# Gate projections in another order, and q's low part written straight into two lasting buffers

## The chip, the cores and the metric

The kernel runs on one core of one Trainium2 chip. The metric is the device time of one execution in microseconds (us); the median of several executions is compared. A profile of one execution shows what each engine did: PE is TensorE (matmuls), PEld its weight loads, DVE VectorE, ACT ScalarE, POOL GpSimd, SP SyncE, which here only issues DMAs.

## What is computed

The block takes x of shape (1, 1024, 1024), with sequence length S = 1024 and width D = 1024:

```python
h = _rmsnorm(x, norm_g)
u = h @ w_in                       # RWKV columns, attention columns, 2048 gate columns
y = wkv7_scan(r, decay, k, v, -kk, kk * a)      # 8 heads of 64, a recurrence over 1024 steps
a_out = (groupnorm(y) + bonus) * silu(gate_a)
q, k = _rmsnorm(q), _rmsnorm(k)                 # 8 heads of 64
logits = q @ k.T * scale + cum[q] - cum[k]      # cum: running sum of log_sigmoid(f)
b_out = softmax(causal(logits)) @ v * silu(gate_b)
m = sigmoid(gate_1) * (a_out @ w_out_a) + sigmoid(gate_2) * (b_out @ w_out_b)
out = _rmsnorm(x + m @ w_out, final_norm_g)
```

Everything is fp32. The matmuls take each operand as a high and a low part (names with H and L): high times high, high times low and low times high, three matmuls for one product.

## The kernel before

**Bulk work.** `project` multiplies one 128-column block of weights with the transposed, normed input `hTH`/`hTL` for one half n of the sequence: 24 matmuls of 512 columns into one PSUM tile. `mix` uses it for RWKV columns (with the token shift), `gate_tile(j)` for the gates: j = 16 to 19 are RWKV's gates and go through `mix`, j = 20 to 23 are attention's gates, j = 0 to 15 the 16 sigmoid gates of the final merge. What must read the PSUM tile before it is free differs. For 0 to 15 it is ACT alone (L413). For 20 to 23 it is ACT and then DVE (L417). For 16 to 19 it is ACT and then DVE (L375 and, for the first half, L381, `last_gg`), with the silu's product (L402) also on DVE. The bulk tiles rotate through three PSUM buffers, so that a tile's first matmul waits for the readers of the tile three before it. Results go to DRAM (`gab`) and come back when they are used. The weights of each block come by DMA (L225, L873, L941) into one raw buffer, are cast by ACT (L210) and their low parts made by POOL (L213).

**RWKV.** Four units (p, n), called 0_0, 0_1, 1_0 and 1_1, run in sequence. `prep` of a unit forms products `psc` (PE, L604), masks them on DVE into QL and Q (L610), scales them on POOL, sends them through DRAM into the layout `lt` (DMAs L639 and L643), inverts a triangular matrix by elimination in some sixty small steps on DVE (L680, L684, with the scratch tile `etmp`), goes through DRAM again, transposes on DVE into `TW` (L696), and multiplies on PE (`pw` L704, `pz` L717). `chain` then runs 8 steps that depend on each other (px, xw, pu, SV, po, state). `norm_out` closes the unit (the gate `yg` is loaded, POOL multiplies, L828). Bulk work lies between these pieces on PE.

**Attention.** Four pairs of heads p. `norm_qk` makes the high parts QA and KA by ACT and the low parts by DVE; QA's second copy is made by DMA (L1010, L1011). q's low part goes from DVE (`ql`, L1004) to DRAM (`qlo`, L1008); `attend` zeroes half of a tile QZ on POOL (L1030) for each of its four blocks of 256 queries and loads the other half from `qlo` (L1031). The scores `sc` are a matmul with QA (L1053), one with QZ (L1056) and a mask (L1060). The probabilities are transposed (pt), split (PHL, L1084 to 1093) and multiplied with V (po, L1099). Beside this PE runs the projections of the next pair (`pf`) and gate tiles.

**Merge.** `ring` tiles bring gates, attention results and weights; `pma` and `pmb` are bulk tiles of the output projections, freed by DVE (L1155, L1158).

**What sets the order.** A scheduler lays every engine's order in advance; each engine then runs its list in that order, and an instruction that waits holds all behind it. `PLACE` pins the first matmuls of a group behind a given count of bulk pieces ("pw1_0": 404 means not before piece 404), `SCAT` does so for the first scores of a pair, `PTAT` for the last unit's transposes. `RFILL` and `FPRE` say how many gate tiles are taken from the list `gates` beside each unit and each attention pair. Tags name memory: tiles of one tag share a buffer, and the later waits for the last reader of the earlier.

Of the kernel before, what the change touches and what calls it, by code (L numbers as in the profile page):

```python
# [9 lines left out]
F32 = mybir.dt.float32  # L10
# [8 lines left out]
P = 128  # L19
# [32 lines left out]
QKFIRST = True  # L52
LATER = 1000000
PLACE = {
    "pw0_0": 179, "pz0_0": 183, "pw0_1": 296, "pz0_1": 301, "sc1_0": 352, "pw1_0": 404, "pz1_0": 409,
    "sc1_1": 457, "pw1_1": 525, "pz1_1": 535,
}
PACE = 0.3
PHPOOL = True
# [38 lines left out]
def kernel(  # L98
# [318 lines left out]
                nc.vector.scalar_tensor_tensor(t, t, 1.0, ps, op0=ALU.add, op1=ALU.mult)  # L417
            store(n, t)

    gates = list(range(16, 24)) + list(range(16))  # L420

    def fill(n, off=LATER):
        with order(off):
# [92 lines left out]
    def prep(pp_, n):  # L516
# [43 lines left out]
        nc.vector.reciprocal(s2c, s2)  # L560

        bo = ep.tile([P, UC, 2, C], F32, tag="prod", name=f"bo{u}")
        late_sc = []
        for e in range(2):
            p, w = 2 * pp_ + e, f"{u}_{e}"
            own, other = (slice(0, C), slice(C, P))[:: 1 - 2 * e]
            ta, th = ew(f"ta{w}"), ew(f"th{w}")
            nc.sync.dma_start(flat(th), lod[0, p, :, HS[n]])
            nc.sync.dma_start(flat(ta), lod[1, p, :, HS[n]])
            sg = ew(f"sg{w}")  # L570
            nc.vector.memset(pad(sg)[:, :, 0:1], 0.0)
            nc.vector.tensor_scalar(pad(sg)[:, :, 1:], ch(th), 0.5, 0.5, op0=ALU.mult, op1=ALU.add)
            cum = ew(f"cum{w}")
            nc.vector.tensor_tensor_scan(
                cum, d0.rearrange("p c t -> p (c t)"), sg, 0.0, op0=ALU.mult, op1=ALU.add
            )
            E = ew(f"E{w}")
            nc.scalar.activation(E, cum, AF.Exp, scale=-KAPPA)
            Ei = ew(f"Ei{w}")
            nc.scalar.activation(ch(Ei), pad(cum)[:, :, 1:], AF.Exp, scale=KAPPA)  # L580
            nc.vector.tensor_copy(WC[:, e], pad(E)[:, :, C])

            BK = ep.tile([P, UC, P], F32, tag="lt", name=f"BK{w}")
# [12 lines left out]
            nc.vector.scalar_tensor_tensor(bo[:, :, e], ch(ta), cs("rk", p), ch(rx[e]), op0=ALU.mult, op1=ALU.mult)


            for h, q in ((0, A), (1, B)):
                for g in range(2):  # L600
                    psc = ps_misc(f"psc{w}_{g}_{h}")
                    for j in range(4):
                        c = 4 * g + j
                        ins = nc.tensor.matmul(  # L604
                            psc[:, j * P : (j + 1) * P], BK[q, c, :], AR[q, e, c, :], start=True, stop=True
                        )
                        if e:
                            late_sc.append(ins.ins)
                    for cols, m, dst in ((own, 0, QL), (other, C, Q)):
                        nc.vector.tensor_mul(  # L610
                            dst[:, e, h, 4 * g : 4 * g + 4, :],
                            psc.rearrange("p (c t) -> p c t", t=P)[:, :, cols],
                            mask[:, m : m + C].unsqueeze(1).broadcast_to([P, 4, C]),
                        )
            for g in range(2):
                pb = ps_misc(f"pb{w}_{g}")
                for j in range(4):
                    nc.tensor.transpose(pb[:, j * P : (j + 1) * P], BK[:, 4 * g + j, :], ident)
                nc.scalar.copy(BKt[:, e, 4 * g : 4 * g + 4].rearrange("p c i -> p (c i)"), pb)
# [52 lines left out]
                        )  # L672
            nc.scalar.copy(AK[:, 4 * g : 4 * g + 4].rearrange("p c i -> p (c i)"), pk)

        etmp = rp.tile([4 * NG, 2, 256], F32, tag="etmp", name=f"etmp{u}")
        nc.vector.memset(lt[:, 0 : HB * HB : HB + 1], 1.0)
        for s in range(1, HB - 1):
            m = HB - 1 - s
# [8 lines left out]
        for e, _, *qs in half:  # L687
            for i, q in enumerate(qs):
                for h in range(2):
                    nc.sync.dma_start(  # L690
                        Tg[q, h, :, q], td[e, i, UC * h : UC * h + UC].transpose([1, 0, 2])
                    )
        TW = rp.tile([P, HALF], F32, tag="TW", name=f"TW{u}").rearrange("p (g t) -> p g t", t=HB)
        for e, _, q1, q2 in half:
            for h in range(2):
                nc.vector.transpose(TW[q1, UC * h : UC * h + UC, :], Tg[q1, h, :, q1])  # L696
# [23 lines left out]
                    )  # L720
        for e, _, q1, q2 in half:
            nc.scalar.copy(Tg[q1, :, :, q2], pz[q1, :].rearrange("p (h c t) -> p h c t", h=2, t=HB))
        return dict(pz=pzs, AR=AR, Q=Q, BKt=BKt, SV=SV, AK=AK, WC=WC, bV=bV, s2c=s2c, lnw=lnw, pw=mms, sc=late_sc, pt=[])

    states = [rp.tile([P, 2, 2, C], F32, tag=f"state{j}", name=f"state{j}") for j in range(2)]
    for t in states:
# [2 lines left out]
    def chain(pp_, n, d):  # L729
# [1 line left out]
        u = f"{pp_}_{n}"  # L731
        pairs = ((0, A, B), (1, B, A))
        yv = rp.tile([P, UC, 2, C], F32, tag="yw", name=f"yv{u}", bufs=YWB)
        xw = rp.tile([P, 4, P], F32, tag="xw", name=f"xw{u}")
        for c in range(UC):
            gc = UC * n + c
            st_c, st_n = states[gc % 2], states[1 - gc % 2]
# [58 lines left out]
    def norm_out(pp_, n, d, yv):  # L796
# [26 lines left out]
                )  # L823
        for e in range(2):
            p = 2 * pp_ + e
            yg = rp.tile([P, HALF], F32, tag="yg", name=f"yg{u}_{e}")
            nc.sync.dma_start(yg, gab[16 + p, :, HS[n]])
            nc.gpsimd.tensor_mul(yo[:, e], yo[:, e], yg)  # L828
            nc.sync.dma_start(yab[p, :, HS[n]], yo[:, e])
# [146 lines left out]
    def norm_qk(p, xn, rr):  # L976
# [2 lines left out]

        KA = (rp if p % 2 else qp).tile([P, 2, S], F32R, tag=("Q", "AR")[p % 2], name=f"KA{p}")  # L980
        QA = rp.tile([P, 2, S], F32R, tag=("QL", "BKt")[p % 2], name=f"QA{p}")
        qlo = dp.tile([P, S], F32, tag="qlo", name=f"qlo{p}", bufs=2)

        def half(n, places):
            xg = xn[n].rearrange("p b (g i) -> p (b g) i", i=HD)
            (nc.gpsimd if n in NORMPOOL else nc.vector).tensor_mul(xg, xg, rr[n].unsqueeze(2).broadcast_to([P, 16, HD]))
            for c, key in ((1, "k"), (0, "q")):
# [7 lines left out]
                hi = KA if key == "k" else QA  # L995
                for h, q, qo in halves:
                    nc.scalar.activation(hi[q, h, HS[n]], pq[q], AF.Copy, scale=1.0 if key == "k" else gqk[q])
                if key == "q":
                    ql = rp.tile([P, HALF], F32R, tag=("TW", "etmp")[n], name=f"ql{p}_{n}")
                for h, q, qo in halves:  # L1000
                    if key == "k":
                        nc.vector.tensor_sub(KA[qo, h, HS[n]], pq[q], hi[q, h, HS[n]])  # L1002
                    else:
                        nc.vector.scalar_tensor_tensor(  # L1004
                            ql[q], pq[q], gqk[q], hi[q, h, HS[n]], op0=ALU.mult, op1=ALU.subtract
                        )
                if key == "q":
                    nc.sync.dma_start(qlo[:, HS[n]], ql.bitcast(F32))  # L1008
            QAf = QA.bitcast(F32)[:, :, HS[n]]
            nc.sync.dma_start(QAf[B, 0], QAf[A, 0])  # L1010
            nc.sync.dma_start(QAf[A, 1], QAf[B, 1])  # L1011

        return KA, QA, qlo, half

    sc_tags = SCTAGS

    blocks = [[] for _ in range(4)]

    def attend(p, KA, QA, qlo):
        cb = [rp.tile([P, S], F32, tag=("AK", "bV")[h], name=f"cb{p}_{h}") for h in range(2)]  # L1020
        for h in range(2):
            src = cumd[8 * (2 * p + h) : 8 * (2 * p + h) + 8].rearrange("(o b) t -> o (b t)", o=1)
            nc.sync.dma_start(cb[h], src.broadcast_to([P, S]))
        for i in range(4):
            nb = 2 * i + 2

            QZ = rp.tile([P, 2, QB], F32R, tag=("yg", "xw")[i % 2], name=f"QZ{p}_{i}")
            QZf = QZ.bitcast(F32)
            for h, q, qo in ((0, A, B), (1, B, A)):
                nc.gpsimd.memset(QZf[qo, h, :], 0.0)  # L1030
                nc.sync.dma_start(QZf[q, h, :], qlo[q, i * QB : (i + 1) * QB])  # L1031
            yo = rp.tile([P, QB], F32, tag="state0", name=f"yo{p}_{i}")
            yg = rp.tile([P, QB], F32, tag="state1", name=f"yg{p}_{i}")
            nc.sync.dma_start(yg, gab[20 + p, :, i * QB : (i + 1) * QB])
            for h, q in ((0, A), (1, B)):
# [3 lines left out]
                for e in range(2):  # L1039
# [6 lines left out]
                    for g in range(ng):  # L1046
# [7 lines left out]
                        if e == 0 and g == 0:  # L1054
                            blocks[p].append(qk.ins)
                        nc.tensor.matmul(  # L1056
                            sc[:, :mw], QZ[:, h, e * P : (e + 1) * P], KA[:, h, ms], start=False, stop=not end
                        )
                        if end:
                            nc.tensor.matmul(sc[:, gw - P : gw], identb, cmask, start=False, stop=True)  # L1060
# [69 lines left out]
    def merge():  # L1130
# [9 lines left out]
        with tc.tile_pool(name="yp", bufs=1, side="right", reuse_waits="tile") as yp:  # L1140
# [46 lines left out]
    for i, (p, n) in enumerate(units):  # L1187
# [3 lines left out]
        with bulky():  # L1191
# [3 lines left out]
            fill(RFILL[i], 0)  # L1195
            if i + 1 == len(units):
                project_v(0)
                forget()
                xr = project_qk(0)
        not_before(d["pw"], f"pw{p}_{n}")  # L1200
        not_before(d["pz"], f"pz{p}_{n}")
        not_before(d["sc"], f"sc{p}_{n}")
        if i:
            not_before(before["pt"], "pt%d_%d" % units[i - 1])
# [9 lines left out]

    def next_qk(p, xr, between=lambda: None):

        KA, QA, qlo, half = norm_qk(p, *xr)
        starts.append(len(laid_) - 1)
        half(0, QKAT[0])
        between()  # L1220
        with order(LATER) if p == 0 else nullcontext():
            gate_tile(gates.pop(0))
        half(1, QKAT[1])
        return KA, QA, qlo

    def last_norm():
        with order(-LATER):
# [15 lines left out]
    for p in range(4):  # L1243
        end = starts[p + 1] if p < 3 else len(laid_) - 1
        room = sum(cols_[starts[p] + 1 : end + 1]) - SCAT * HALF
        for k, first in enumerate(blocks[p]):
            i, h = divmod(k, 2)
            if k == 0 or SPREAD:
                pins.append(([first], starts[p], int(SCAT * HALF + SPREAD * room * (i + h) * (i + 1) / 20)))
    bulk_tags[:] = TTAGS  # L1250
    tc.cur_priority += LATER
    place_all()
    mH, mL, wos = merge()
# [65 lines left out]
```

## Time and profile before

| | |
|---|---|
| median of 3 runs | 1120.16 us (1118.36 to 1122.01) |
| the profiled execution | 1110.45 us |
| its span in the profile | 1108.4 us |
| mean granted clock of TensorE | 0.981 of full speed |
| busy: PE, DVE, ACT, POOL | 1044.7, 703.9, 460.1, 320.9 us |

The span is what the profile covers; the 2 us beside it lie before and after. The profiled execution was 9.7 us shorter than the median of the timed runs.

### The profile page before, as it was taken

How to read it: one execution, taken by the hardware profiler on the slowest of the kernel's cores; microseconds unless marked ns; L12 is line 12 of the kernel's file. 1: busy time of each engine (PE TensorE's matmuls, PEld its weight loads, DVE VectorE, ACT ScalarE, POOL GpSimd, SP SyncE). 2: the span in 40 equal slices, each digit the busy share in tenths (PEclk: the TensorE clock that was granted, in tenths of full speed). 3: DMA queues.
4: the chain of work that ended last, by engine and by line, in shares of the span. 5: the costliest groups of instructions: out<-in, count | busy, mean ns of one | idle time of the engine just before them, and what ended most of it. 6: DMA issues, size and time to landing. Idle time of an engine off the chain costs nothing. (4 is left out here: it accounts for less than half of the span.)

```text
span 1108.4 us, 18398 instructions
## 1 busy us (share of the span) xinstructions
PE 1044.7 (94%) x6591; PEld 866.8 (78%) x6591; DVE 703.9 (64%) x1855; ACT 460.1 (42%) x969; POOL 320.9 (29%) x467
## 2 busy tenths in 40 slices
PE   4989999998999998999989899899999899999996
PEld 3867788776778776778979788787899687887885
DVE  7414775699737873597466595785764685475145
ACT  6545323533243323423353564665453563233122
POOL 4531522234222531143120422323222322335300
PEclk9999999999999899999979899999999999999999
DMA  6266434224522343223211512313232416645133
GB/s 218 56 185 219 133 96 124 62 74 121 146 89 60 114 126 113 59 56 107 71 39 51 153 51 76 106 48 97 63 109 58 130 51 205 192 141 190 51 102 123
DMA packets 126685, 118.21 MB, mean 107 GB/s; under 512 B 33490, under 2 KB 91971, under 8 KB 126595
## 3 DMA queue, kind: packets, MB, share of 16 engines
q1 hardware_dynamic: 114304, 94.99, 29.6%
q10 hardware_dynamic: 11714, 21.52, 5.2%
q8 instruction: 52, 0.85, 0.3%
q0 software_dynamic: 576, 0.54, 0.2%
q14 instruction: 39, 0.31, 0.1%
HBM read 79.23 MB, written 35.68 MB: 104 GB/s over the span
## 5 line engine op out<-in xcount | busy, mean ns | idle before, releaser
L348 PE MATMUL ps_gg<-hTH,wH_gg 128*128 128x512 f32 x384 | 159.3, 415 | 7.0 <-DVE last_gg L381 4.4
L350 PE MATMUL ps_gg<-hTH,wL_gg 128*128 128x512 f32 x384 | 156.6, 408 | 0.0
L349 PE MATMUL ps_gg<-hTL,wH_gg 128*128 128x512 f32 x384 | 156.1, 406 | 0.0
L213 POOL TENSOR_TENSOR wL_gg<-w_gg,wH_gg 128x256 fp32r<-128x256 f32 x96 | 75.3, 815 | 191.6 <-ACT wH_gg L210 146.0
L348 PEld LDWEIGHTS ps_gg<-hTH,wH_gg 128*128 128x128 f32 x384 | 73.4, 191 | 24.1 <-issue 5.4
L350 PEld LDWEIGHTS ps_gg<-hTH,wL_gg 128*128 128x128 f32 x384 | 73.3, 191 | 14.9
L349 PEld LDWEIGHTS ps_gg<-hTL,wH_gg 128*128 128x128 f32 x384 | 73.4, 191 | 14.0
L959 PE MATMUL pf<-wqkH,hTH 128*128 128x256 f32 x256 | 74.7, 292 | 0.2 <-DVE KA L1002 0.2
L960 PE MATMUL pf<-wqkL,hTH 128*128 128x256 f32 x256 | 74.6, 291 | 0.0
L961 PE MATMUL pf<-wqkH,hTL 128*128 128x256 f32 x256 | 74.4, 291 | 0.0
L758 ACT ACTIVATE xw<-state,WC 64x64 f32<-64x64 f32 x112 | 38.9, 348 | 44.0 <-DVE state L778 34.7
L1066 ACT ACTIVATE pr<-pr,mm 128x128 f32<-128x128 f32 (+3 forms) x64 | 50.0, 782 | 17.2 <-DVE mm L1062 16.4
L680 DVE TENSOR_TENSOR etmp<-lt 64x30 f32<-64x30 f32 (+14 forms) x120 | 47.8, 398 | 10.7 <-issue 7.1
L1062 DVE CUSTOM_DVE_ANT_0 pr<-sc,cb 128x128 f32<-128x128 f32 (+3 forms) x64 | 34.0, 534 | 30.8 <-PE sc L1060 24.1
L413 ACT ACTIVATE gt<-ps_gg 128x512 f32<-128x512 f32 x40 | 23.9, 599 | 70.8 <-PE ps_gg L350 63.5
L1273 PE MATMUL pz<-wo,mH 128*128 128x512 f32 (+1 forms) x136 | 51.9, 382 | 0.9 <-POOL wo L1128 0.9
L1274 PE MATMUL pz<-wo,mL 128*128 128x512 f32 (+1 forms) x136 | 52.3, 385 | 0.0
L1272 PE MATMUL pz<-wo,mH 128*128 128x512 f32 (+1 forms) x136 | 51.7, 380 | 0.0
L684 DVE TENSOR_TENSOR lt<-lt,etmp 64x30 f32<-64x30 f32 (+14 forms) x120 | 48.3, 402 | 3.6
L959 PEld LDWEIGHTS pf<-wqkH,hTH 128*128 128x128 f32 x256 | 49.7, 194 | 0.6 <-DVE KA L1002 0.4
L1099 PE MATMUL po<-PHL,V 128*128 128x256 f32 x160 | 46.8, 307 | 2.9 <-ACT PHL L1084 2.7
L960 PEld LDWEIGHTS pf<-wqkL,hTH 128*128 128x128 f32 x256 | 49.4, 193 | 0.0
(332 smaller groups left out, 2826.9 us busy)
## 6 DMA issues: line engine op xcount, KB each, us to landing
w_gg<-in_w_in_dram SPq DMA_DIRECT2D x24, 512.0 KB, 3.8
gab<-gt ACTq DMA_DIRECT2D x48, 256.0 KB, 2.3
ring<-gab SPq DMA_DIRECT2D x32, 256.0 KB, 3.2
xt<-in_x_dram SPq DMA_DIRECT2D x8, 512.0 KB, 5.8
wqk<-in_w_in_dram SPq DMA_DIRECT2D x16, 256.0 KB, 3.1
cb<-cumd SPq DMA_DIRECT2D x8, 512.0 KB, 4.1
ring<-yab SPq DMA_DIRECT2D x16, 256.0 KB, 3.5
ring<-in_w_out_dram SPq DMA_DIRECT2D x16, 256.0 KB, 2.8
```

The costliest lines, as they stand in the source:

```text
L213: nc.gpsimd.tensor_sub(wL[:, k], w[:, k], wH[:, k])
L348: nc.tensor.matmul(ps, wH[:, k, :], rH[:, k, ts_], start=(k == 0), stop=False)
L349: nc.tensor.matmul(ps, wH[:, k, :], rL[:, k, ts_], start=False, stop=False)
L350: laid(nc.tensor.matmul(ps, wL[:, k, :], rH[:, k, ts_], start=False, stop=(k == nk - 1)))
L684: nc.vector.tensor_add(lt3[:, :s, s + 1 :], lt3[:, :s, s + 1 :], tm)
L959: nc.tensor.matmul(ps, hTH[:, k, bs], wH[:, kk, :], start=(k == 0), stop=False)
L960: nc.tensor.matmul(ps, hTH[:, k, bs], wL[:, kk, :], start=False, stop=False)
L961: laid(nc.tensor.matmul(ps, hTL[:, k, bs], wH[:, kk, :], start=False, stop=(k == KD - 1)), QB)
L1066: nc.scalar.activation(pr[:, :w], pr[:, :w], AF.Exp, bias=last, scale=-1.0, accum_out=mm[:, 2:3])
L1272: nc.tensor.matmul(ps, mH[:, k, bs], oH[:, k, c], start=(k == 0), stop=False)
L1273: nc.tensor.matmul(ps, mH[:, k, bs], oL[:, k, c], start=False, stop=False)
L1274: nc.tensor.matmul(ps, mL[:, k, bs], oH[:, k, c], start=False, stop=(k == KD - 1))
```

## The change

The list of gates gets another order, and one gate tile is taken between v's projection and those of q and k for the last unit. Pins and counts change with it. `etmp` and `TW` become one tile (`inv`), `xw` and `yg` another (`xy`). DVE writes q's low part straight into two tiles `QZ` that take over these tags once; their other rows are zeroed once, for pair 0. The DRAM tensor `qlo`, its 8 stores, 32 loads and 32 zeroings are gone. The tag list `TTAGS` (8 PSUM buffers for bulk tiles) is set after the `pma` tiles, no longer before them; until then `FTAGS` (3 buffers) holds.

```diff
-    "pw0_0": 179, "pz0_0": 183, "pw0_1": 296, "pz0_1": 301, "sc1_0": 352, "pw1_0": 404, "pz1_0": 409,
-    "sc1_1": 457, "pw1_1": 525, "pz1_1": 535,
+    "se0_0": 113, "pw0_0": 179, "pz0_0": 183, "pw0_1": 296, "pz0_1": 301, "sc1_0": 356, "pw1_0": 408, "pz1_0": 413,
+    "sc1_1": 461, "pw1_1": 540, "pz1_1": 548,
...
-PTAT = 6
-SCAT = 16
+PTAT = 5
+SCAT = 14
...
-RFILL = [5, 5, 4, 4]
-FPRE = [0, 0, 0, 2]
+RFILL = [5, 5, 4, 3]
+FPRE = [0, 0, 1, 1]
...
-    gates = list(range(16, 24)) + list(range(16))
+    gates = [16, 17, 0, 1, 2, 3, 18, 19, 4, 5, 6, 7, 20, 21, 22, 23] + list(range(8, 16))
...
-        etmp = rp.tile([4 * NG, 2, 256], F32, tag="etmp", name=f"etmp{u}")
+        inv = rp.tile([P, 2, HALF], F32, tag="inv", name=f"inv{u}")
+        etmp = inv[: 4 * NG, 0].rearrange("p (a b) -> p a b", a=2)
...
-        qlo = dp.tile([P, S], F32, tag="qlo", name=f"qlo{p}", bufs=2)
...
-                if key == "q":
-                    ql = rp.tile([P, HALF], F32R, tag=("TW", "etmp")[n], name=f"ql{p}_{n}")
+                if p == 0 and key == "q":
+                    QZ.append(rp.tile([P, 2, HALF], F32R, tag=("inv", "xy")[n], name=f"QZ{n}"))
+                    for h, q, qo in halves:
+                        nc.gpsimd.memset(QZ[n].bitcast(F32)[qo, h, :], 0.0)
...
-                            ql[q], pq[q], gqk[q], hi[q, h, HS[n]], op0=ALU.mult, op1=ALU.subtract
+                            QZ[n][q, h, :], pq[q], gqk[q], hi[q, h, HS[n]], op0=ALU.mult, op1=ALU.subtract
...
-                if key == "q":
-                    nc.sync.dma_start(qlo[:, HS[n]], ql.bitcast(F32))
...
-            QZ = rp.tile([P, 2, QB], F32R, tag=("yg", "xw")[i % 2], name=f"QZ{p}_{i}")
-            QZf = QZ.bitcast(F32)
-            for h, q, qo in ((0, A, B), (1, B, A)):
-                nc.gpsimd.memset(QZf[qo, h, :], 0.0)
-                nc.sync.dma_start(QZf[q, h, :], qlo[q, i * QB : (i + 1) * QB])
+            QZi = QZ[i // 2][:, :, (i % 2) * QB : (i % 2 + 1) * QB]
...
+            bulk_tags[:] = TTAGS
             for c in range(KD):
                 side(w_out_b, yb, 4, "b", c, then_b)
...
                 project_v(0)
+                gate_tile(gates.pop(0))
                 forget()
                 xr = project_qk(0)
...
-    bulk_tags[:] = TTAGS
     tc.cur_priority += LATER
     place_all()
```

The laid order on DVE during the elimination of unit 0_1, before the change; `ps_gg_1978` is the first half of gate 18:

```order
L680 TENSOR_TENSOR etmp_1_2706<-lt_1_2634 64x220
L684 TENSOR_TENSOR lt_1_2634<-lt_1_2634,etmp_1_2706 64x20x11
L375 SCALAR_TENSOR_TENSOR gt_0_2005<-ps_gg_1978,col,t_gg_2003 128x511
L680 TENSOR_TENSOR etmp_1_2706<-lt_1_2634 64x210
L378 SCALAR_TENSOR_TENSOR gt_0_2005<-zcol,col,t_gg_2003 128x1
L684 TENSOR_TENSOR lt_1_2634<-lt_1_2634,etmp_1_2706 64x21x10
L381 COPY last_gg_2008<-ps_gg_1978 128x1
L680 TENSOR_TENSOR etmp_1_2706<-lt_1_2634 64x198
L402 SCALAR_TENSOR_TENSOR gt_0_2005<-gth_0_2010,gt_0_2005 128x512
L684 TENSOR_TENSOR lt_1_2634<-lt_1_2634,etmp_1_2706 64x22x9
```

The same steps of the elimination after the change, where the gate in that place is gate 0:

```order
L680 TENSOR_TENSOR inv_1_2673<-lt_1_2601 64x220
L684 TENSOR_TENSOR lt_1_2601<-lt_1_2601,inv_1_2673 64x20x11
L680 TENSOR_TENSOR inv_1_2673<-lt_1_2601 64x210
L684 TENSOR_TENSOR lt_1_2601<-lt_1_2601,inv_1_2673 64x21x10
L680 TENSOR_TENSOR inv_1_2673<-lt_1_2601 64x198
L684 TENSOR_TENSOR lt_1_2601<-lt_1_2601,inv_1_2673 64x22x9
L680 TENSOR_TENSOR inv_1_2673<-lt_1_2601 64x184
L684 TENSOR_TENSOR lt_1_2601<-lt_1_2601,inv_1_2673 64x23x8
```

The five DVE instructions of a `mix` gate between the steps have left this stretch; gates 18 and 19 now come four gates later, after 0 to 3.

PE where the chain of unit 1_1 runs and the first `pf` of q and k comes, before the change:

```order
L746 MATMUL px_1_4_5706<-state_432,AR_1_4373 128x128 x2
L761 MATMUL pu_1_4_5717<-xw_1_5595,Tb 128x64 x2
L771 MATMUL po_1_4_5722<-SV_1_4377,BKt_1_4376 128x128 x2
L746 MATMUL px_1_5_5729<-state_433,AR_1_4373 128x128 x2
L918 MATMUL pcs<-lf,tri 128x64
L919 MATMUL pcs<-lf,tri 128x64
L761 MATMUL pu_1_5_5740<-xw_1_5595,Tb 128x64 x2
L771 MATMUL po_1_5_5745<-SV_1_4377,BKt_1_4376 128x128 x2
L746 MATMUL px_1_6_5752<-state_432,AR_1_4373 128x128 x2
L761 MATMUL pu_1_6_5763<-xw_1_5595,Tb 128x64 x2
L959 MATMUL pf_0_1_5365<-wqkH_0_5314,hTH 128x256
```

And after it; `ps_gg_1_5248` is the second half of the gate tile that now stands between v and q and k:

```order
L348 MATMUL ps_gg_1_5248<-hTH,wH_gg_5211 128x512
L349 MATMUL ps_gg_1_5248<-hTL,wH_gg_5211 128x512
L350 MATMUL ps_gg_1_5248<-hTH,wL_gg_5212 128x512
L772 MATMUL po_1_2_5648<-SV_1_4364,BKt_1_4363 128x128 x2
L919 MATMUL pcs<-lf,tri 128x64
L920 MATMUL pcs<-lf,tri 128x64
L747 MATMUL px_1_3_5655<-state_433,AR_1_4360 128x128 x2
L762 MATMUL pu_1_3_5666<-xy_1_5585,Tb 128x64 x2
L772 MATMUL po_1_3_5671<-SV_1_4364,BKt_1_4363 128x128 x2
L788 MATMUL py_1_3_5678<-SV_1_4364,Q_1_4361 64x64 x16
L747 MATMUL px_1_4_5696<-state_432,AR_1_4360 128x128 x2
L762 MATMUL pu_1_4_5707<-xy_1_5585,Tb 128x64 x2
```

What has no bulk between it, before, are the chain's pieces from po_1_3 to pu_1_6 (po_1_3 and py_1_3 stand just ahead of these rows), and after the change those from po_1_2 to pu_1_4.

SP before the scores of pair 3, before the change (`w_gg` is a gate's weights, `w_oa` those of merge):

```order
L1010 DMA QA_8833<-QA_8833 64x512
L1011 DMA QA_8833<-QA_8833 64x512
L225 DMA w_gg_9529<-in_w_in_dram 128x8x128
L1008 DMA qlo_8834<-ql_0_8852 128x512
L1031 DMA QZ_0_8950<-qlo_8834 64x256 x2
L1031 DMA QZ_1_9034<-qlo_8834 64x256 x2
```

And after it:

```order
L225 DMA w_gg_8841<-in_w_in_dram 128x8x128
L225 DMA w_gg_9423<-in_w_in_dram 128x8x128
L1011 DMA QA_8817<-QA_8817 64x512
L1012 DMA QA_8817<-QA_8817 64x512
L234 DMA w_oa_9528<-in_w_out_a_dram 128x4x256
```

The store of `qlo` and the loads of QZ are gone from the queue, and so is the load of a gate's weights in front of them; merge's weights follow QA's copies directly.

## Rows read from the trace of the kernel before

**Rows 1.** The page, part 1: busy time, share of the span and instructions of each engine.

```profile
PE 1044.7 (94%) x6591; PEld 866.8 (78%) x6591; DVE 703.9 (64%) x1855; ACT 460.1 (42%) x969; POOL 320.9 (29%) x467
```

**Rows 2.** The waits of PE: total us, times, longest; after the arrow what ended them.

```profile
PE sc L1056 <- DMA QZ<-qlo: 10.9, 5, 3.2
...
PE ps_gg L348 <- DVE last_gg L381: 4.4, 2, 3.0
...
PE psc L604 <- DVE Q L610: 3.0, 2, 2.0
PE pw L704 <- DVE TW L696: 2.8, 2, 1.5
PE po L1099 <- ACT PHL L1084: 2.7, 2, 2.1
PE ps_gg L348 <- DVE gt L375: 1.6, 2, 1.2
...
PE ps_gg L348 <- DVE gt L417: 0.9, 1, 0.9
```

**Rows 3.** Windows of DVE: us and length, DVE busy (x instructions), PEclk, DMA share, GB/s.

```profile
240.00:270.00 30.00, 28.94 (x70) 0.97 0.37 96
...
313.00:350.00 37.00, 21.32 (x66) 1.00 0.28 87
...
350.00:370.00 20.00, 19.81 (x38) 1.00 0.33 97
```

**Rows 4.** Windows of PE: us and length, PE busy (x instructions), PEclk, DMA share, GB/s.

```profile
370.00:380.00 10.00, 8.00 (x47) 0.87 0.46 151
380.00:390.00 10.00, 9.71 (x78) 0.79 0.33 68
563.00:568.60 5.60, 4.12 (x50) 1.00 0.02 4
568.60:582.20 13.60, 10.72 (x44) 0.50 0.31 80
620.00:630.00 10.00, 6.82 (x32) 0.66 0.44 134
860.00:870.00 10.00, 7.37 (x51) 1.00 0.38 120
```

**Rows 5.** Timeline of PE where prep's matmuls stand: start, us, line, tile [idle before].

```profile
376.15 1.01 PE L604 MATMUL psc<-AR,BK 64*128 64x128 f32 x7 [2.00 <-DVE Q L610]
...
426.87 0.69 PE L704 MATMUL pw<-TW,Tb 32*32 32x32 f32 x32 [1.28 <-DVE TW L696]
...
541.55 1.13 PE L704 MATMUL pw<-TW,Tb 32*32 32x32 f32 x59
```

**Rows 6.** Timeline of SP, 387 to 388 us: when each DMA is issued.

```profile
387.38 0.38 SPq L524 DMA_DIRECT2D vx<-xd  x1
387.93 0.47 SPq L643 DMA_DIRECT2D lt<-ld  x1
```

**Rows 7.** Timeline of SP before the scores of pair 3.

```profile
855.66 0.39 SPq L225 DMA_DIRECT2D w_gg<-in_w_in_dram  x1
...
861.01 2.40 SPq L1031 DMA_DIRECT2D QZ<-qlo  x4
```

**Rows 8.** Timeline of PE at the first scores of pair 3.

```profile
860.40 0.28 PE L1053 MATMUL sc<-KA,QA 128*128 128x256 f32 x1
863.31 0.40 PE L1056 MATMUL sc<-KA,QZ 128*128 128x256 f32 x1 [2.63 <-DMA QZ<-qlo]
```

**Rows 9.** Timeline of DVE in merge: the additions L1155 that free the PSUM of pma.

```profile
947.63 1.28 DVE L1155 SCALAR_TENSOR_TENSOR m<-ring,pma 128x512 f32<-128x512 f32 x2
...
953.26 1.28 DVE L1155 SCALAR_TENSOR_TENSOR m<-ring,pma 128x512 f32<-128x512 f32 x2
...
961.40 0.69 DVE L1155 SCALAR_TENSOR_TENSOR m<-ring,pma 128x512 f32<-128x512 f32 x1 [2.11 <-PE pma L350]
964.20 0.69 DVE L1155 SCALAR_TENSOR_TENSOR m<-ring,pma 128x512 f32<-128x512 f32 x1 [2.11 <-PE pma L350]
```

More of the change, by code (lines that the diff above doesn't have):

```diff
@@ L562, in prep @@
         bo = ep.tile([P, UC, 2, C], F32, tag="prod", name=f"bo{u}")
-        late_sc = []
+        first_sc, late_sc = [], []
         for e in range(2):
@@ L606, in prep @@
                         )
-                        if e:
-                            late_sc.append(ins.ins)
+                        (late_sc if e else first_sc).append(ins.ins)
                     for cols, m, dst in ((own, 0, QL), (other, C, Q)):
@@ L692, in prep @@
                     )
-        TW = rp.tile([P, HALF], F32, tag="TW", name=f"TW{u}").rearrange("p (g t) -> p g t", t=HB)
+        TW = inv[:, 1].rearrange("p (g t) -> p g t", t=HB)
         for e, _, q1, q2 in half:
@@ L722, in prep @@
             nc.scalar.copy(Tg[q1, :, :, q2], pz[q1, :].rearrange("p (h c t) -> p h c t", h=2, t=HB))
-        return dict(pz=pzs, AR=AR, Q=Q, BKt=BKt, SV=SV, AK=AK, WC=WC, bV=bV, s2c=s2c, lnw=lnw, pw=mms, sc=late_sc, pt=[])
+        return dict(pz=pzs, AR=AR, Q=Q, BKt=BKt, SV=SV, AK=AK, WC=WC, bV=bV, s2c=s2c, lnw=lnw, pw=mms, se=first_sc, sc=late_sc, pt=[])
     states = [rp.tile([P, 2, 2, C], F32, tag=f"state{j}", name=f"state{j}") for j in range(2)]
@@ L733, in chain @@
         yv = rp.tile([P, UC, 2, C], F32, tag="yw", name=f"yv{u}", bufs=YWB)
-        xw = rp.tile([P, 4, P], F32, tag="xw", name=f"xw{u}")
+        d["xy"] = rp.tile([P, 2, HALF], F32, tag="xy", name=f"xy{u}")
+        xw = d["xy"][:, 0].rearrange("p (a b) -> p a b", a=4)
         for c in range(UC):
@@ L825, in norm_out @@
             p = 2 * pp_ + e
-            yg = rp.tile([P, HALF], F32, tag="yg", name=f"yg{u}_{e}")
+            yg = d["xy"][:, 1]
             nc.sync.dma_start(yg, gab[16 + p, :, HS[n]])
@@ L1011, in half, with attend @@
             nc.sync.dma_start(QAf[A, 1], QAf[B, 1])
-        return KA, QA, qlo, half
+        return KA, QA, half
     sc_tags = SCTAGS
+    QZ = []
     blocks = [[] for _ in range(4)]
-    def attend(p, KA, QA, qlo):
+    def attend(p, KA, QA):
         cb = [rp.tile([P, S], F32, tag=("AK", "bV")[h], name=f"cb{p}_{h}") for h in range(2)]
@@ L1056, in attend @@
                         nc.tensor.matmul(
-                            sc[:, :mw], QZ[:, h, e * P : (e + 1) * P], KA[:, h, ms], start=False, stop=not end
+                            sc[:, :mw], QZi[:, h, e * P : (e + 1) * P], KA[:, h, ms], start=False, stop=not end
                         )
@@ L1201 @@
         not_before(d["pz"], f"pz{p}_{n}")
+        not_before(d["se"], f"se{p}_{n}")
         not_before(d["sc"], f"sc{p}_{n}")
@@ L1215, in next_qk @@
     def next_qk(p, xr, between=lambda: None):
-        KA, QA, qlo, half = norm_qk(p, *xr)
+        KA, QA, half = norm_qk(p, *xr)
         starts.append(len(laid_) - 1)
@@ L1223, in next_qk @@
         half(1, QKAT[1])
-        return KA, QA, qlo
+        return KA, QA
     def last_norm():
```

## The prediction

> **What bounds the kernel now.** I read the page first. PE is busy for 1044.7 of 1108.4 us [rows 1]; no other engine is near that. So time can only be won where PE stands still or runs slowly, and PE's bulk work, which the change does not touch in amount, lies in a fixed order. The list of PE's waits comes next. Its largest entry is the scores' second matmul, waiting for a DMA: 10.9 us in five places, 3.2 us the longest. Then come the gates' PSUM tiles, whose readers on DVE are late (4.4, 1.6 and 0.9 us), `psc` behind DVE's Q (3.0), `pw` behind TW (2.8) and `po` behind PHL (2.7) [rows 2]. The windows of PE then show what a stop costs beside its own length. The granted clock was 0.87 and 0.79 between 370 and 390 us, 0.50 from 568.6 to 582.2, and 0.66 from 620 to 630 us, but 1.00 from 860 to 870 us, although PE was busy for only 7.37 of those 10 us [rows 4]. Last I looked at what is late behind each wait: DVE is busy for 28.94 of the 30 us from 240 to 270 and for 19.81 of the 20 from 350 to 370, but only for 21.32 of the 37 us from 313 to 350 [rows 3].
>
> **The change part by part.** All terms are in us of the profiled execution; plus is time won.
>
> *Gates 0 to 3 ahead of 18 and 19.* The bulk that lies beside unit 0_1's elimination is freed by ACT alone, where before DVE had to find room for five instructions of each half gate among the elimination's steps. The first wait of 3.0 us belongs to gate 17, which stays; the waits for gates 18 and 20 go: 4.4 − 3.0 = 1.4 for `last_gg`, 1.2 for L375, 0.9 for L417 [rows 2]. That is 3.5. Gates 18 and 19 themselves now lie where DVE has 16 us of 37 free [rows 3]. Upper bound 3.9 (all of L375's 1.6), lower bound 2, if one wait like the 1.4 comes back there. I take **+3.5**.
>
> *Unit 1_0.* Its pins move by 4 pieces, and the last gate of the moved pair puts some of its DVE work into the stretch that is already full [rows 3]. PE comes to `psc` later against its bulk, so the 2.00 us there [rows 5] shrink, and with them the slow clock behind it: 10 × 0.13 + 10 × 0.21 = 3.4 us between 370 and 390 [rows 4]. But `pw`, which waited 1.28 us at its last piece [rows 5] and 2.8 in all with the one before [rows 2], is set by a serial path: Q, POOL, a DMA, the elimination, a DMA, TW. PE that is faster in between only waits there longer. The path shortens only where PE itself is in it: `lt`'s load stands on SP behind a load of `vx` at 387.38 that follows a product of PE [rows 6], and that product comes earlier by what the slow clock took. So between 0 and 3.4; I take **+2**.
>
> *Unit 1_1.* In the laid order PE has, between its `psc` and its `pw`, about 12 matmuls of 512 columns fewer than before, and `pw` had no wait at 541.55 [rows 5]. Twelve such matmuls are one tile of merge, which takes 964.20 − 961.40 = 2.8 us [rows 9]. PE can thus come up to 2.8 us early to a TW that is no earlier, and `lt`'s load now stands behind one more weight load on SP. Between −3 and 0; I take **−1.5**. The pin of unit 0_0's first `psc` I cost at nothing: no `psc` wait but those at Q appears in the list, and only a few bulk matmuls change sides with it.
>
> *One gate tile between v and q and k.* In unit 1_1 the chain's pieces have no bulk beside them from po_1_3 to pu_1_6, some two and a half steps; after the change from po_1_2 to pu_1_4, one step less, and the gate tile lies beside the steps before. From 563.0 to 582.2 PE was idle for 1.5 + 2.9 = 4.4 us and did 10.72 us of work at half clock, which is 5.4 us too long [rows 4]: 9.8 together. Three fifths of the bare stretch remain. If the clock falls as before, 0.4 × 9.8 = 3.9 is won; if it holds, 9.8 − 0.6 × 4.4 = 7.2. I take **+5**.
>
> *q's low part in place, first pair.* The first wait of 3.2 goes [rows 2], and the slow clock behind it: 0.34 of 6.82 us busy, or 2.3 [rows 4]. DVE's write is the same instruction as before with another target, and the DMA store, the load and the zeroing behind it leave the path. **+5.5**; 6.6 if the clock's loss counts over all 10 us, 3.2 if it stays.
>
> *The same, pairs 1 to 3.* The other four waits: 10.9 − 3.2 = 7.7 [rows 2]. What is late next are the copies of QA. At pair 3 the matmul with QA ran at 860.40 without a wait, 2.9 us before the one with QZ [rows 8], whose loads were issued only at 861.01, behind a weight load at 855.66 [rows 7]. With SCAT at 14 the scores start two pieces sooner, 6 matmuls or 1.4 us by the tile above. I take **+7**, with 4 and 7.7 as bounds. The lasting tiles cost no wait of their own: on PE more than 200 rows of the laid order stand between the last scores that read one and the next pair's q.
>
> *Merge with 3 PSUM buffers for `pma`.* A tile of 2.8 us must be freed within the 5.6 us that the next two take. The longest distance between two frees was 953.26 − 947.63 = 5.6 us, and near the end each came with its tile [rows 9]. Between −3 (three late frees of 1 us) and 0; I take **−1**.
>
> The sum is 3.5 + 2 − 1.5 + 5 + 5.5 + 7 − 1 = 20.5. Against it stands what no row can show: each stop also let ACT, DVE and POOL catch up, and the order behind it is fixed. At ten places where a stop goes I put half of one of the smaller waits in the list (0.9) [rows 2], some 5 us, with 0 and 10 as bounds. That leaves **15 us**. On the profiled execution's 1110.45 this gives 1095.5; that execution was 9.7 us below the median of the runs, so against the median, 1120.16, I forecast **1105**. With the forecast's terms at their ends, its own range is 1096 to 1112.
>
> **Clock, rule and row.** The first pair's wait was followed by a clock of 0.66, the last pair's of nearly the same length by 1.00 [rows 4]. The Trainium skill ("TensorE: Matmul & The Clock Gate", "HAM oscillation — how this bites in real kernels") describes a kernel in which each wait for a DMA makes the next group of matmuls start at the slow clock. By that rule four more losses like the 2.3 of the first pair would be won back, and the sum would be 9 higher. The trace speaks against it at 860, so it stands among the rivals with a small chance.
>
> **The rivals.**
> - *The scores wait for QA's copies instead* (chance 0.10). For it: the copies are DMAs on the same queue, and the scores start 1.4 us sooner. Against it: 860.40 had no wait [rows 8]. Then the 7 us of pairs 1 to 3 and up to half of the first pair's are lost: 4 to 8 us won, 1112 to 1116.
> - *The gates' waits only move* (0.10). For it: DVE has no room from 350 to 370 [rows 3], and TW's path is serial. Then the first three terms turn from +4 to −4, and 7 us are left: 1113.
> - *Every wait also costs clock* (0.05), also in the rows where the windows show 1.00: four times the first pair's 2.3 come on top, 9 us, 1096.
> - *Both of the first two together* (0.07). The change then does what it says on paper, but every wait is replaced: 15 − 11 − 4, no change, about 1120.
> - *Slower: `pma` starves on 3 buffers* (0.08). `pma` now begins while the last pair's attention still fills DVE and SP. If DVE's additions come later than 5.6 us after their tile, PE pays the excess each time. To eat 15 us and more, each of the 16 tiles must be freed about 1 us too late; at 1.5 us each, 24 us are lost: 1129. The longest distance in the rows, 5.6 us, lies just at the limit, but stands once [rows 9].
>
> **How the numbers follow.** The forecast holds 0.60. 0.3% (3.4 us) is about what a measurement can tell from no change. Faster by more: 0.60 + 0.10 + 0.10 + 0.05 = 0.85. Within it: 0.07. Slower: 0.08. The range must reach to the cases on the faster side, up to 1116, and down to where the clock comes back as well; 1094 to 1117 leaves out the last two rivals and a few per cent below.
>
> **What would show it.** Right: no wait of the scores for a DMA of QZ, a clock near 1.00 after the first scores and around the former 370 to 390; no wait for `last_gg` but gate 17's; PE idle in the last chain about half as long; `pw` of unit 1_0 with a longer wait than 2.8 us. Wrong: scores waiting for QA, `pma` waiting for the additions that free it, `pw` of unit 1_1 waiting more than 3 us, or a new wait above 2 us inside attention.

## The result

The changed kernel takes 1105.64 us (median of 4 runs, 1103.19 to 1107.51) against 1119.26 us (4 runs, 1117.84 to 1122.01): ratio 0.9879, 95% interval 0.9847 to 0.9911, or 13.6 us less. The forecast was 1105. The number came out within 1 us, in part by luck: the terms of units 1_0 and 1_1 were off by 12.7 us together, and the discount for what no row showed, the other terms and the scatter between executions made up for it.

**The profile after.** The profiled execution took 1103.19 us, its span 1101.5. The page's busy times (part 1):

```profile
PE 1036.6 (94%) x6591; PEld 859.8 (78%) x6591; DVE 707.7 (64%) x1855; ACT 457.3 (42%) x969; POOL 310.8 (28%) x439
```

The list of PE's waits, as in [rows 2]: total, times, longest.

```profile
PE pfv L890 <- DVE lf L901: 10.7, 1, 10.7
...
PE psc L604 <- DVE Q L609: 4.2, 2, 3.3
...
PE ps_gg L348 <- DVE last_gg L381: 2.8, 1, 2.8
...
PE pw L704 <- DVE inv L696: 2.1, 2, 1.8
PE ps_gg L348 <- DVE gt L375: 1.7, 2, 1.3
...
PE sc L1050 <- DVE mm L1059: 1.5, 5, 0.5
```

The scores wait for no DMA any more; what remains for them is 1.5 us in five pieces, for a PSUM tile. Of the waits for gates the one for gate 17's first half (2.8) is left; 1.3 for L375 at its second half and 0.7 for ACT (L413) behind it are new. But a wait that the kernel before did not have is now the longest behind the start-up: 10.7 us in one piece, `pfv`, the projection of v, for DVE's `lf`. Windows of PE, as in [rows 4]:

```profile
380.00:390.00 10.00, 9.05 (x38) 0.52 0.18 49
530.00:540.00 10.00, 2.27 (x10) 0.50 0.13 27
540.00:550.00 10.00, 10.00 (x72) 0.84 0.18 28
...
570.00:580.00 10.00, 8.31 (x68) 0.87 0.42 116
580.00:590.00 10.00, 8.95 (x67) 0.96 0.07 20
620.00:630.00 10.00, 9.60 (x54) 1.00 0.65 199
...
860.00:870.00 10.00, 9.55 (x50) 1.00 0.26 79
```

Around the first scores PE is busy for 9.60 us of ten at a clock of 1.00, where it had 6.82 and 0.66 [rows 4], and around pair 3's for 9.55 instead of 7.37. The chain's clock is 0.87 and 0.96 instead of 0.50. From 380 to 390 it is 0.52, lower than before, and the new stop has its own slow clock behind it. What stands before the former is `psc` in unit 1_0, as in [rows 5]:

```profile
380.95 3.75 PE L604 MATMUL psc<-AR,BK 64*128 64x128 f32 x16 [3.27 <-DVE Q L609]
```

**Where the time went.** Matmuls that stand behind the same bulk work in both orders, counted in columns, can be compared by their starts in the two traces. (For unit 1_1 that means 48 gate matmuls of 512 columns fewer and 93 of v's, with 264 columns, more.)

| start of | before | after | after − before | won since the line above |
|---|---|---|---|---|
| first `pw` of unit 0_0 | 180.41 | 184.16 | +3.75 | (start-up) |
| first `pw` of unit 0_1 | 308.78 | 309.00 | +0.22 | 3.5 |
| first `pw` of unit 1_1 | 541.55 | 553.92 | +12.37 | −12.2 |
| first `pqk` of pair 0 | 604.34 | 610.84 | +6.50 | 5.9 |
| first `pqk` of pair 1 | 679.99 | 680.98 | +0.99 | 5.5 |
| first `pqk` of pair 2 | 752.53 | 750.38 | −2.15 | 3.1 |
| first `pmb` of merge | 964.00 | 957.39 | −6.61 | 4.5 |
| first matmul of the last output tile | 1096.99 | 1090.07 | −6.92 | 0.3 |

The 3.75 us at the top are start-up ahead of anything that the change does in this trace; behind them the changed kernel wins 10.7 us.

**The new wait.** PE around it:

```profile
518.08 0.29 PE L890 MATMUL pfv<-wvH,hTH 128*128 128x264 f32 x1
...
526.76 0.28 PE L892 MATMUL pfv<-wvH,hTL 128*128 128x264 f32 x1
537.73 0.56 PE L890 MATMUL pfv<-wvH,hTH 128*128 128x264 f32 x1 [10.69 <-DVE lf L901]
```

DVE in the same stretch, by its timeline:

```profile
512.41 0.14 DVE L680 TENSOR_TENSOR inv<-lt 64x30 f32<-64x30 f32 x1 [3.71 <-issue]
...
523.70 0.83 DVE L680 TENSOR_TENSOR inv<-lt 64x240 f32<-64x240 f32 x1
...
536.79 0.20 DVE L684 TENSOR_TENSOR lt<-lt,inv 64x30 f32<-64x30 f32 x1
...
537.03 0.49 DVE L899 TENSOR_TENSOR V<-pfv,V 128x128 fp32r<-128x128 f32 x2
537.43 0.15 DVE L901 TENSOR_TENSOR lf<-pfv,fb 128x8 f32<-128x8 f32 x1
```

And ACT:

```profile
523.18 0.42 ACT L895 CAST V<-pfv 128x128 fp32r<-128x128 f32 x2
```

ACT had copied the first tile of v from PSUM at 523.18. DVE's reading of the same tile (L899 and, the last, L901) stands in its list behind the elimination of unit 1_1, whose last step starts at 536.79. Three PSUM buffers were full, so the fourth tile waited for 10.69 us, until 537.73. In the kernel before, one gate tile more lay ahead of v, 48 matmuls or 11 us at 2.8 for 12 [rows 9], and PE reached `pw` at 541.55 without a wait [rows 5]. The first matmul of v and the elimination's first and last steps, in the kernel before:

```profile
530.54 0.28 PE L889 MATMUL pfv<-wvH,hTH 128*128 128x264 f32 x1
```

```profile
507.25 0.28 DVE L680 TENSOR_TENSOR etmp<-lt 64x30 f32<-64x30 f32 x1
...
532.35 0.20 DVE L684 TENSOR_TENSOR lt<-lt,etmp 64x30 f32<-64x30 f32 x1
```

So two things met. PE came to v 12.5 us earlier (518.08 instead of 530.54), nearly all of it by the gate that was moved away, and the elimination ended 4.4 us later (536.79 instead of 532.35 for its last step). By these numbers the move alone would have left a stop of some 6 us (10.7 − 4.4). That is an estimate; no run moved the gate with the elimination where it had been. `lt`'s load was issued at 507.91 instead of 502.83. About half of that comes with `psc`, which PE began 2.5 us later (475.37 instead of 472.89) because the pins put more bulk ahead of it; the rest arises between DVE's masks and the load. The extra gate between v and q and k was not an added one: RFILL had given it up ahead of v.

### The profile page after: what moved, and what is told of

Same layout as the page of the kernel before. It is cut to its first block, busy times and chain, and to the rows that moved or that the text cites. A ratio compares the mean times of both kernels' runs of the same rounds, so it can differ in the third digit from the quotient of the medians.

```text
span 1101.5 us, 18278 instructions
## 1 busy us (share of the span) xinstructions
PE 1036.6 (94%) x6591; PEld 859.8 (78%) x6591; DVE 707.7 (64%) x1855; ACT 457.3 (42%) x969; POOL 310.8 (28%) x439
## 5 line engine op out<-in xcount | busy, mean ns | idle before, releaser
L680 DVE TENSOR_TENSOR inv<-lt 64x30 f32<-64x30 f32 (+14 forms) x120 | 47.9, 399 | 15.0 <-issue 11.4
L413 ACT ACTIVATE gt<-ps_gg 128x512 f32<-128x512 f32 x40 | 23.9, 597 | 72.9 <-PE ps_gg L350 47.2
L759 ACT ACTIVATE xy<-state,WC 64x64 f32<-64x64 f32 x112 | 38.7, 345 | 35.1 <-DVE state L779 22.6
L890 PE MATMUL pfv<-wvH,hTH 128*128 128x264 f32 (+1 forms) x128 | 38.5, 301 | 11.3 <-DVE lf L901 10.7
L1076 PE MATMUL pt<-ident,pr 128*128 128x128 f32 x288 | 46.4, 274 | 2.5 <-DVE pr L1067 2.5
L962 PEld LDWEIGHTS pf<-wqkH,hTL 128*128 128x128 f32 x256 | 48.3, 189 | 0.0
```

What stands on the lines that cost most here:

```text
L680: nc.vector.tensor_mul(tm, lt3[:, s, s + 1 :].unsqueeze(1).broadcast_to([4 * NG, s, m]), lt3[:, :s, s].unsqueeze(2).broadcast_to([4 * NG, ...
L962: laid(nc.tensor.matmul(ps, hTL[:, k, bs], wH[:, kk, :], start=False, stop=(k == KD - 1)), QB)
```

## The experiments

All times below are medians; the ratio is to the kernel before on the same chip.

**q_alone.** The kernel before, with the lasting QZ tiles and the two shared tags alone:

```diff
-                    ql = rp.tile([P, HALF], F32R, tag=("TW", "etmp")[n], name=f"ql{p}_{n}")
+                    QZ.append(rp.tile([P, 2, HALF], F32R, tag=("inv", "xy")[n], name=f"QZ{n}"))
```

> The kernel before with one part of the change alone: q's low part written straight into the two lasting tiles (with the shared tags it needs). Gate order, gate counts, pins, SCAT, PTAT and merge's buffers are as before. Theory A (the waits for QZ and the slow clock behind the first of them were PE's own lost time): the scores wait for no DMA, the first pair wins about 5 us and the others 7, so 1105 to 1109. Theory B (the scores then wait for QA's copies, and the gain of the whole change came from the gates): 1114 to 1120, with waits of the scores' first matmul above 1 us each.

Measured: 1109.78 us, ratio 0.9909 (0.9880 to 0.9937), 10.0 us less. The scores' waits for QZ are gone; QA's copies cost 0.4 us, once. That is theory A, just above its range: a wait of `po` for PHL came at 639.04, with a clock of 0.83 from 640 to 650 us. In this trace the first pair wins 3.0 us against the kernel before (first `pqk` of pair 0 to that of pair 1), not the 5 of theory A.

```profile
639.04 0.39 PE L1096 MATMUL po<-PHL,V 128*128 128x256 f32 x1 [1.61 <-ACT PHL L1086]
```

**q_undone.** The changed kernel with q's low part through DRAM again (the lines of the diff on QZ, `ql` and `qlo` undone).

> The changed kernel with q's low part sent through DRAM again, all the rest of the change kept. Theory A (the gates' part of the change wins 3.5 us beside unit 0_1, loses about 2.6 in unit 1_0 and 10 in the new wait of v's projection, and wins 7 in the chain and 1 to 2 in merge): 1116 to 1122, that is, no clear change against the kernel before. Theory B (the gates' part carries the gain): 1106 to 1111.

Measured: 1128.17 us, ratio 1.0074 (1.0047 to 1.0102), 8.4 us more than before. Both theories missed. PE's waits:

```profile
PE sc L1055 <- DMA QZ<-qlo: 19.2, 8, 3.7
...
PE pfv L888 <- DVE lf L899: 10.9, 1, 10.9
```

The DRAM path had become dearer, 19.2 us in eight places instead of 10.9 in five [rows 2]. So the run taught that the parts of the change don't add up, and asked what made the path dearer.

**q_undone_s16.** As q_undone, with the scores' start as before:

```diff
-PTAT = 5
-SCAT = 14
+PTAT = 6
+SCAT = 16
```

> The run q_undone (the changed kernel with q's low part through DRAM) with SCAT at 16 and PTAT at 6, as before the change. Theory A (the scores' earlier start is what made the DRAM path dearer there, 19.2 us of waits in eight places instead of 10.9 in five): the waits for QZ fall back to 10 to 13 us and the time to 1119 to 1123. Theory B (the waits grew because the queue around the stores and loads has another order, or because PE is earlier for the other reasons): they stay above 17 us and the time at 1126 to 1130.

Measured: 1119.40 us, ratio 1.0011 (0.9996 to 1.0025).

```profile
PE pfv L888 <- DVE lf L899: 10.7, 1, 10.7
PE sc L1055 <- DMA QZ<-qlo: 10.6, 6, 3.6
```

Theory A by the waits and the time. Two steps of SCAT (and one of PTAT, which the runs don't separate) cost 0.63% by the ratios, 7 us, where the scores wait for two DMAs in a row. The run also gives the value of all that the change does besides q and the scores' start: nothing that can be told from zero. What it wins beside unit 0_1 and in the chain, the wait of 10.7 us takes back, as the table above shows for the changed kernel.

**noextra.** The changed kernel with the gate put back ahead of v:

```diff
-    ... "pw1_1": 540, "pz1_1": 548,
+    ... "pw1_1": 525, "pz1_1": 535,
-RFILL = [5, 5, 4, 3]
+RFILL = [5, 5, 4, 4]
                 project_v(0)
-                gate_tile(gates.pop(0))
```

> The changed kernel with its extra gate tile put back from behind v's projection to in front of it (RFILL 4 instead of 3; the pins pw1_1 and pz1_1 at 525 and 535, so that the same bulk lies ahead of pw). Theory A (v's first tiles come 16 bulk pieces too early, while DVE's copies of them are laid behind the elimination): the wait of 10.7 us for lf and the half clock behind it are gone, about 13 us, and the bare chain with its 9 us of idle time and slow clock is back: 1100 to 1104. Theory B (the elimination of unit 1_1 itself is late, whatever bulk lies beside it, because its load stands behind another on SP's queue): the same time is waited at pw, and the bare chain comes on top: 1110 to 1114.

Measured: 1106.96 us, ratio 0.9882 (0.9852 to 0.9911), the same as the changed kernel, between the two theories.

```profile
PE pw L704 <- DVE inv L696: 4.1, 3, 1.6
...
PE pfv L890 <- DVE lf L901: 2.1, 1, 2.1
```

The wait for `lf` did shrink to 2.1 us, as A has it, but `pw` of unit 1_1 now waits too (1.61 us at 547.78; the other 2.5 belong to unit 1_0), so theory B has its share: the elimination's last step starts at 541.77 here, 9.4 us later than before, though the bulk ahead of v and `pw` is that of the kernel before (PE itself was 1.5 us behind at the first `pw` of unit 0_1). A slow clock stands around these two short stops, and again in the bare chain:

```profile
540.00:550.00 10.00, 6.27 (x45) 0.69 0.50 106
550.00:560.00 10.00, 10.00 (x157) 0.63 0.01 2
...
580.00:590.00 10.00, 7.25 (x28) 0.56 0.36 103
590.00:600.00 10.00, 10.00 (x89) 0.75 0.23 71
```

**cover.** The changed kernel with a gate ahead of v and the extra one behind it, and one fewer beside the last pair of attention (pair 3, which the expectation calls the third):

```diff
-RFILL = [5, 5, 4, 3]
-FPRE = [0, 0, 1, 1]
+RFILL = [5, 5, 4, 4]
+FPRE = [0, 0, 1, 0]
```

> The changed kernel with one gate tile more ahead of v's projection (RFILL 4) and one fewer beside the third attention pair (FPRE 0, 0, 1, 0); the extra gate behind v stays. Bulk now lies beside the elimination and beside the whole last chain. Theory A (two separate lacks of cover): the wait for lf and its slow clock are gone and the chain is not bare at all, 12 to 16 us less than the changed kernel, 1090 to 1095. Theory B (attention needs the gate that is taken from it, or pw waits instead): at most 4 us less, 1101 to 1107, with new waits in the last pairs or at pw.

Measured: 1094.37 us, ratio 0.9780 (0.9752 to 0.9807), 11.3 us less than the changed kernel: theory A. `lf` costs 2.7 us in two places, and the clock holds from 530 us on through the last unit's chain. The elimination's last step starts at 538.89, no earlier than in the changed kernel; there is now work beside it. As the pins of the changed kernel stay, 15 pieces of v's projection (45 matmuls, some 5 us) lie ahead of `pw` beyond those in noextra, so cover differs from noextra in more than the gate behind v:

```profile
PE pfv L890 <- DVE lf L901: 2.7, 2, 1.9
```

```profile
540.00:550.00 10.00, 9.22 (x128) 1.00 0.50 107
...
570.00:580.00 10.00, 10.00 (x84) 1.00 0.27 80
580.00:590.00 10.00, 9.75 (x96) 1.00 0.23 71
```

**g_alone.** The kernel before with the new list of gates alone (the one line of the diff).

> The kernel before with the new list of gates alone. Theory A (what is won beside unit 0_1 is given back in unit 1_0, where the moved gates fill DVE ahead of the masks): the waits at gates 18 and 20 go, 3.5 us, the wait of psc in unit 1_0 grows from 2.0 to 3 or more with a slower clock behind it, and the time is 1117 to 1121, no clear change. Theory B (the given-back part in the changed kernel came from the moved pins): the 3.5 us stay, 1114 to 1117.

Measured: 1123.32 us, ratio 1.0039 (1.0019 to 1.0059), by the ratio 4.4 us more: worse than either theory. The waits at gates 18 and 20 are gone, and `psc` waits longer, as A has it. What A lacked is unit 1_1, where `pw` waits (2.6 of the 6.2 us below) and the clock falls to 0.73 from 550 to 560 us. From its first `pw` to the first `pqk` of pair 0 PE takes 68.3 us, where the kernel before took 62.8:

```profile
PE pw L704 <- DVE TW L696: 6.2, 5, 2.3
PE psc L604 <- DVE Q L610: 4.5, 2, 2.9
...
PE ps_gg L348 <- DVE last_gg L381: 3.0, 1, 3.0
```

**cover_old.** cover with the old list of gates.

> The run cover with the old list of gates (16 to 23, then 0 to 15). Theory A (with the elimination and the chain covered, the list matters little: 3.5 us are lost again beside unit 0_1, and 3 to 5 come back in units 1_0 and 1_1): 1093 to 1097. Theory B (the list is what makes the cover work): 1099 to 1104.

Measured: 1104.18 us, ratio 0.9874 (0.9856 to 0.9893), some 10 us more than cover: theory B, just past its upper end. The old list brings back the two gates' waits and, in unit 1_0, one for DVE:

```profile
PE ps_gg L348 <- DVE last_gg L381: 4.7, 2, 2.8
PE pt L819 <- DVE yv L814: 4.0, 1, 4.0
```

So the same line costs 4.4 us in the kernel before and saves 10 in cover. The traces suggest why, though no run isolates it: where the last unit has no spare bulk, PE that comes earlier only stops there.

**cover_sc.** cover with unit 1_0's pins later:

```diff
-    "sc1_0": 356, "pw1_0": 408, "pz1_0": 413,
+    "sc1_0": 362, "pw1_0": 414, "pz1_0": 419,
```

> The run cover with the three pins of unit 1_0 six pieces later, so that PE has some 4 us more bulk ahead of psc. Theory A (PE's stop for psc is PE's own lost time): the stop of 3.3 us and the half clock from 380 to 390 go, and the wait at pw does not grow by as much: 1088 to 1092. Theory B (DVE's serial path from the masks to TW sets when the unit ends): nothing is won, 1093 to 1097, and pw waits longer or the chain is later.

Measured: 1095.03 us, ratio 0.9802 (0.9779 to 0.9825), no different from cover: theory B. PE stops for as long at nearly the same time, before another matmul that needs DVE (cover stopped for 3.26 us, until 380.66, at `psc`):

```profile
382.26 1.02 PE L819 MATMUL pt<-ident,yv 128*128 128x128 f32 x7 [3.21 <-DVE yv L814]
```

**t_back and cover_t.** The changed kernel, and cover, with `bulk_tags[:] = TTAGS` back ahead of merge.

> The changed kernel with merge's first tiles on the 8 PSUM buffers again. Theory A (three buffers cost little, as forecast, 0 to 3 us): 1103 to 1106. Theory B (they hold PE back where merge begins beside the last pair): 4 us or more less, 1099 to 1102, with fewer waits between 900 and 930 us.

> The run cover with merge's first tiles on the 8 PSUM buffers again. If the three buffers hold PE back a little where merge begins, as t_back suggested, the 2 to 3 us come on top: 1090 to 1093. If that difference was only the scatter between runs: 1093 to 1096.

Measured: t_back 1102.46 us, ratio 0.9859 (0.9840 to 0.9879); cover_t 1092.99, ratio 0.9783 (0.9768 to 0.9798). The intervals overlap with those of the changed kernel and of cover (0.9780); that the time of cover_t lies in the lower of its two ranges says little, because the kernel before was 2.4 us faster beside it (1117.45) than beside cover (1119.80). In the trace of t_back v's wait is 9.0 us instead of 10.7, a difference that lies ahead of merge. Three buffers or eight make no difference here that these runs can tell.

The best of the versions are cover and cover_t, 2.2% under the kernel before and 1% under the changed one by the ratios.

## Why the prediction was right, and where it was not

**Gates 0 to 3 beside unit 0_1: +3.5, measured 3.5** (the second line of the table). The stop for gate 17 stays and those for 18 and 20 go, as it was put. That the number fits to the tenth is luck in this trace: the two new stops of 1.29 and 0.70 us came in, so the stops on this stretch fell from 6.5 to 4.8 us only, by 1.7. About as much came from the clock behind gate 17's stop, which the term did not count. PE there before, and then after:

```profile
268.50:275.00 6.50, 6.47 (x22) 0.76 0.13 45
```

```profile
272.00:279.00 7.00, 5.83 (x24) 1.00 0.19 52
```

In t_back, which has the same order there, the clock was 0.76 again behind a stop of 2.82 us, the only other new stop was 0.65 us, and the stretch won 3.7. So the size holds; the sum that gave it does not quite. (By the order shown above DVE has four instructions for the first half of such a gate, L375, L378, L381 and L402, not five; the second half has no L381.)

**Unit 1_0 and unit 1_1: +2 and −1.5, measured −12.2 together.** This is the step that failed, in unit 1_1 above all. At the first `psc` of unit 1_1 (472.89 before, 475.37 after) the changed kernel is 2.5 us behind with 11 gate matmuls more done, 2.6 us at 2.8 for 12 [rows 9]. So unit 1_0 came to about nothing, and nearly the whole loss is unit 1_1's. In unit 1_0 the stop at `psc` did not shrink but grew, from 2.00 us [rows 5] to 3.3, with a clock of 0.52 behind it: PE came there 3.5 us later, but DVE's masks released it 4.8 us later, at 380.95 instead of 376.15 [rows 5]. `pw` waited less there, 2.1 in all, not more as forecast. cover_sc shows that DVE sets the time there: bulk put ahead only moves the stop. In unit 1_1 I looked for the missing cover at `pw`, at up to 3 us, and took TW as no earlier. But PE first came to PSUM tiles whose readers stand behind the elimination in DVE's order, it came there 12.5 us early, and the elimination was 4.4 us late. `pw` of unit 1_1 itself did not wait. noextra and cover show that the cover is what counts: with a gate more ahead of v the wait falls from 10.7 to 2.1 and 2.7 us. That v's copies laid between the elimination's steps would do the same was not tried, so that half of the explanation rests on the two timelines alone; nor was the elimination's own delay tried by itself.

**The chain: +5, measured 5.9** (the fourth line). The bare stretch got shorter and the clock nearly held (0.87 and 0.96), which lies between my two bounds of 3.9 and 7.2.

**The first pair: +5.5, measured 5.5** (but 3.0 in q_alone, with the same direct write), and **pairs 1 to 3 with merge: +7 − 1, measured 3.1 + 4.5 = 7.6**. The rival of QA's copies did not come: q_alone has 0.4 us of it. (Its own sum, 15 − 7 − 2.75 with half of the first pair lost, gives 5 to 8 us won, not 4 to 8.) But half of the reason that I gave was too simple. I counted SCAT's two steps only as a risk for the copies. By q_undone and q_undone_s16 they cost 7 us with the DRAM path in place; the direct write saves 10.0 us by itself, and with it the earlier start meets no wait for a DMA.

**The discount of 5 us for waits elsewhere** I had spread over ten places. What it stood for came at one place, the projection of v, and twice as large: 3.5 − 12.2 + 5.9 + 5.5 + 7.6 = 10.3 us, where the terms without the discount gave 20.5. By the medians the gain is 13.6; in the two traces, start-up aside, 10.7, and the two profiled executions differ by only 7.3 (1110.45 and 1103.19). The forecast took 15 us off the profiled execution and then added the 9.7 us by which that one lay under the median, so 1105 is near the median in part because the executions scatter. The slower rival, `pma` on three buffers, did not come: no wait of `pma` stands in the list, and t_back and cover_t agree.

**Clock.** I gave the case that every wait for QZ costs clock 0.05, because after 2.63 us of idle time at 860 the clock stayed at 1.00 [rows 4, 8]. In q_undone a wait of nearly that length did cost clock, and so did one of 2.38 us at 730.09. PE's timeline at the first, and the windows behind both:

```profile
700.54 0.58 PE L1055 MATMUL sc<-KA,QZ 128*128 128x256 f32 x1 [2.69 <-DMA QZ<-qlo]
```

```profile
700.00:710.00 10.00, 9.46 (x43) 0.66 0.26 75
730.00:740.00 10.00, 9.91 (x61) 0.83 0.06 15
```

So the Trainium skill's account ("TensorE: Matmul & The Clock Gate", "HAM oscillation — how this bites in real kernels"), that waits for a DMA make the matmuls behind them start slowly, is told of a kernel with waits of about 3 to 5 us; here it holds for some stops of 2.4 to 3.2 us and not for others.

## What to carry to other kernels

When a tile of covering work is moved behind another stage, look up what it covered: here the elimination on DVE lost 11 us of bulk beside it, and the next stage's PSUM readers stood behind it in DVE's fixed order. Cost a wait at the first instruction that depends on the late engine in any way, a full PSUM rotation included, not at the one that needs the late result. And test parts of a change in both surroundings: the list of gates cost 4.4 us alone and saved 10 where the last unit was covered.

## What the runs showed of the hardware

The length of a stop alone does not tell whether the clock falls behind it: 2.63 us before 863 in the kernel before left it at 1.00 [rows 4, 8], 2.69 us before 700.54 in q_undone brought 0.66 for the next ten. Even the same stop in the same order went both ways: 2.83 us at 272.06 in the changed kernel left 1.00, 2.82 us at 271.95 in t_back brought 0.76 from 272 to 279 us.

DVE's small two-operand steps doubled in length while POOL subtracted weights. POOL's timeline in the changed kernel:

```profile
523.35 3.50 POOL L213 TENSOR_TENSOR wL_gg<-w_gg,wH_gg 128x256 fp32r<-128x256 f32 x4 [8.38 <-ACT wH_gg L210]
```

DVE's, at 64x238 just before and right behind that stretch, and at 64x240 inside of it:

```profile
523.27 0.40 DVE L684 TENSOR_TENSOR lt<-lt,inv 64x238 f32<-64x238 f32 x1
...
524.56 0.83 DVE L684 TENSOR_TENSOR lt<-lt,inv 64x240 f32<-64x240 f32 x1
...
526.29 0.82 DVE L684 TENSOR_TENSOR lt<-lt,inv 64x240 f32<-64x240 f32 x1
527.15 0.40 DVE L680 TENSOR_TENSOR inv<-lt 64x238 f32<-64x238 f32 x1
```

From 523.70 to 527.11 each step took 0.82 to 0.83 us, before and after it 0.40. POOL was slower too: four such subtractions with DVE nearly idle beside them took 2.81 us, here 3.50.

```profile
557.92 2.81 POOL L213 TENSOR_TENSOR wqkL<-wqk,wqkH 128x256 fp32r<-128x256 f32 x4 [30.22 <-ACT wqkH L210]
```

The Trainium skill ("SBUF — State Buffer", "SBUF: two separate sides") names the port that DVE and POOL share and says that one holds it for a whole instruction while the other is blocked. The trace agrees that each holds the other up. It does not show them one after the other: the four steps and the four subtractions would then need 1.6 + 2.8 = 4.4 us, and they were done in some 3.8 (523.35 to 527.11).
